# Two-request attention and gMLP encoder: rotary score passes over 128 rows, s tiles in natural order, weight sums spread differently

## The chip, the cores and the metric

The kernel runs on one core of one Trainium2 chip. The time is that of one execution on the device in microseconds (us); the median of several runs is given. The engines of the core work side by side: TensorE (PE in the profile), VectorE (DVE), ScalarE (ACT), GpSimd (POOL), and SyncE (SP), whose queue issues every DMA of this kernel. Each executes its own instructions strictly in the order in which they were written into its queue.

## The reference

Two batches, a sample of 1024 tokens and a prompt of 512 tokens (1024 features each), go through the same two layers. The first layer is multi-head latent attention, the second a gated MLP with a spatial product over chunks of 128 tokens. All is float32.

```python
def mla_layer(x, g, w_in, q_norm, kv_norm, w_q_up, w_kv_up, w_out):
    h = rmsnorm(x, g)
    q_lat, kv_lat, k_rope, gate = jnp.split(h @ w_in, [384, 640, 704], axis=-1)
    q = (rmsnorm(q_lat, q_norm) @ w_q_up).reshape(bsz, seq, 8, 128 + 64)
    kv = (rmsnorm(kv_lat, kv_norm) @ w_kv_up).reshape(bsz, seq, 8, 128 + 128)
    q_rope, k_rope = apply_rope(q[..., 128:], cos, sin), apply_rope(k_rope, cos, sin)
    s = einsum('bqhd,bkhd->bhqk', q_nope, k_nope) + einsum('bqhr,bkr->bhqk', q_rope, k_rope)
    o = einsum('bhqk,bkhd->bqhd', softmax(s * scale), v)
    return x + (o * silu(gate)) @ w_out

def gmlp_layer(x, g, w_in, ln_g, ln_b, w_s, b_s, w_out):
    u, v, gate = jnp.split(rmsnorm(x, g) @ w_in, 3, axis=-1)
    u, v = gelu(u), layernorm(gelu(v), ln_g, ln_b)
    s = u * (einsum('gpq,bnqgd->bnpgd', w_s, v_chunks) + b_s)
    return x + (s * silu(gate)) @ w_out
```

A final RMSNorm follows. The rotary part of a key has 64 features and is shared by the 8 heads.

## The kernel before

**Numbers and products.** Features lie on the partitions and tokens along the free axis. Every float32 operand x of a large product is split into a high part (`split`: a copy by ACT in the rounded type fp32r) and a low part (x minus the high part, by DVE), and a product is made as three matmuls, high*high, high*low and low*high, which add up in one PSUM bank (`mm3`). A matmul has 128 contracted rows and 512, 384 or 256 columns.

**Stages.** In the order of time: the sample's in-projection, the sample's attention (from about 180 us), the prompt's in-projection (about 575 to 660 us), the prompt's attention (to about 770 us), the two attention outputs, and then the gMLP twice, for two groups G=0 and G=1 of 768 tokens each. In a group the products with the weights follow a scheme in which operand blocks are added and subtracted first, and fewer block products are made. Its sums of the weight blocks `wv` are prepared by `w_sums`, eight units (two halves vu, four kt): a unit loads 1 MB into the tile `ws` (`load`, L847), makes four DVE subtractions or additions of 128x512 (`make`, L853) and stores 1 MB to DRAM (L234). Four units (vu=0) lie in the prompt's in-projection, one unit for each two steps of that stage; the other four lie in the attention output.

**Order.** There is no automatic scheduler in this program: each stage is a list of steps written by hand, and extra steps are woven in at positions by number. The order in which steps are called is the order on every engine. `Weights.reach` (L55, L63, L64) loads and splits weights a given number of steps ahead. The function `pin` returns its argument and does nothing else. Buffers are tiles of pools; a tile that lies where an earlier tile lay waits until the last use of the earlier tile is over.

**Scores** (`scores`, L618 to L625). For a block of 128 queries and each of two halves of 512 score columns four matmuls are made over 128 rows: three for the 128 ordinary features, and a fourth for the rotary features, with `qr` holding the high part of the 64 rotary rows in one half of the partitions and the low part in the other, against `krh`, which holds the high key part in both halves. What is then missing is high query times low key, 64 rows only. It is made for both halves together at the end: two matmuls of 64 rows, on rows 0 to 63 and on rows 64 to 127. Since an odd half needs the high part in the other partitions, `qrx` keeps a swapped copy (L582, ACT, 24 copies of 64 rows). The tables cos and sin are loaded by each rotary step (`p_qr`, L561).

**Rotary key of the prompt** (`evac`, f=5): kr from PSUM (L354), loads of cos and sin (L356, L357), four DMAs that shuffle kr into `rope` (L361), kr*cos (L362), rope*sin (L363), their sum (L364), then split into krh and krl.

**Norms in the prompt's in-projection.** Two sums of squares are turned into scales by matmuls on a tile of ones (`ones_mm`, L179 and L180: high part sh, low part sl). The scale is put on a diagonal (`norm_d`, L193, tile `dg`) and split in turn, so that PE waits for ACT's `sh<-dg` and DVE's `sl<-dg`.

**s tiles.** At the end of a group its 16 products s (one for each 128 features, d = 0 to 15) go to DRAM from the tiles `uo` (L234, `sd<-uo`), come back for 512 tokens at a time (L1182), and are split into sh and sl (L1191 by ACT, L1192 by DVE) for the output product (`out`, L1271 to L1273), which takes d in rising order. Tiles 0 to 2 have space of their own. For tiles 3 to 15 space is handed out by `open_out` in this order:

```python
        n = NPRE[G]
        for d in (*range(n + 3, n + 12), *range(n, n + 3), *range(n + 12, 16)):
            s_tiles(G, d)
```

With n = 3 that is 6 to 14, then 3, 4, 5, then 15. The first nine pairs lie where the pool `h2b` was (the split inputs gbh, gbl of the last weight products L1007 to L1009), the later ones where the pool `pu` was, that is the tiles `uo`.

Of the kernel before, what the change touches and what calls it, by code (L numbers as in the profile page):

```python
# [9 lines left out]
F32 = mybir.dt.float32  # L10
# [78 lines left out]
def trunk_kernel(tc, A):  # L89
# [146 lines left out]
    def pin(ins):  # L236

        return ins
# [13 lines left out]
    def setup():  # L252
# [8 lines left out]
        dve.memset(ones[:, :128], 1.0)  # L261
        st["onesr"] = const.tile([128, 128], F32R, name="onesr")
# [250 lines left out]
    def attention(b, n_ch):  # L513
# [5 lines left out]
        def begin():  # L519
            st["at", b] = open_pool("att" + b)  # L520
# [28 lines left out]
        def p_qr(p, c):  # L549
            cc = slice(c * C, (c + 1) * C)  # L550

            def f1():
# [5 lines left out]
                for nm in ("cos", "sin"):  # L558
                    st[nm] = tmp(nm) if n_ch == 1 else st["at", b].tile(
                        [128, C], F32, tag=nm, bufs=1, name=nm)  # L560
                    nc.sync.dma_start(out=st[nm], in_=A[nm][:, cc])  # L561
# [6 lines left out]
            def f2():  # L568
                qx, qs = st["qx"], st["qs"]
                dve.tensor_tensor(out=qx, in0=qx, in1=st["cos"], op=ALU.mult)  # L570
                dve.tensor_tensor(out=qs, in0=qs, in1=st["sin"], op=ALU.mult)

            def f3():
                qr = st["qx"]
                dve.tensor_tensor(out=qr, in0=qr, in1=st["qs"], op=ALU.add)

                x = st["qrx", p, c] = st["at", b].tile([128, C], F32R, tag="qrx", bufs=n_ch, name="qrx")
                for e in range(2):
# [3 lines left out]
                    act.copy(x[o:o + 64], qr[s:s + 64])  # L582
# [21 lines left out]
        def scores(i):  # L604
# [3 lines left out]
            last = []  # L608
            for j2 in range(2):
# [230 lines left out]
    def w_sums(u):  # L840


        vu, kt = divmod(u, 4)

        def load():
            t = st["wsum", u] = st["ws"].tile([128, 4, C], F32, tag="ws", bufs=2 - vu, name="ws")
            nc.sync.dma_start(out=t, in_=A["wv"][vu][:, :, kt, :])  # L847

        def make():
            t = st.pop(("wsum", u))  # L850
            for r, a, b, op in ((3, 2, 3, ALU.add), (2, 0, 2, ALU.subtract),
                                (0, 3, 0, ALU.subtract), (1, 1, 0, ALU.subtract)):
                pin(dve.tensor_tensor(out=t[:, r, :], in0=t[:, a, :], in1=t[:, b, :], op=op))  # L853
            store(st["Sv", vu][:, :, kt, :], t)
# [55 lines left out]
    def b_prep(G):  # L910
# [4 lines left out]
        def load(k):  # L915
            def fn():
                Q[k] = st["hq"].tile([128, 4, H], F32, name=f"hQ{k}")
                for j in range(2):
                    pin(nc.sync.dma_start(out=Q[k][:, j:j + 3:2, :], in_=st["x1d", G, k + 4 * j].rearrange(
                        "p (a b) -> p a b", a=2)))  # L920
# [30 lines left out]
        def first(k):  # L951
            def fn():
                q = Q[k]
                for j in range(2):
                    pin(dve.scalar_tensor_tensor(
                        out=q[:, j:j + 3:2, :], in0=q[:, j:j + 3:2, :],
                        scalar=vec(V_NG1 + k + 4 * j), in1=st["rbc1", G],
                        op0=ALU.mult, op1=ALU.mult))
# [5 lines left out]
        def second(k):  # L964
            def fn():
                q = Q[k]
                dve.tensor_tensor(out=q[:, 2, :], in0=q[:, 3, :], in1=q[:, 2, :], op=ALU.subtract)
# [4 lines left out]
        def third(k):  # L972
            def fn():
                q = Q[k]
                x = tmp("t1")[:, :H].unsqueeze(1)
                dve.tensor_tensor(out=x, in0=q[:, 3:4, :], in1=q[:, 0:1, :], op=ALU.subtract)
# [11 lines left out]
        def fifth(k):  # L988
            def fn():
                q = Q[k]  # L990
                dve.tensor_tensor(out=q[:, 1, :], in0=q[:, 1, :], in1=q[:, 0, :], op=ALU.subtract)
# [91 lines left out]
    def b_ug(G, early):  # L1083
# [4 lines left out]
        def norm_v(p):  # L1088
            def fn():
                v = st["vin", p]  # L1090
                for tt in range(6):
                    pin(dve.tensor_scalar(
                        out=v[:, tt, :], in0=v[:, tt, :], scalar1=st["mv"][:, tt, 0:1],
                        scalar2=st["mv"][:, tt, 3:4], op0=ALU.subtract, op1=ALU.mult))
# [90 lines left out]
    def s_split(g, d):  # L1185
        def fn():
# [4 lines left out]
            pin(act.copy(hi, x))  # L1191
            pin(dve.tensor_tensor(out=lo, in0=x, in1=hi.bitcast(F32), op=ALU.subtract))  # L1192
# [8 lines left out]
    def b_out(g, extra, last):  # L1201
# [24 lines left out]
        def fin4(f):  # L1226
            y = st["yl", f]
            pin(dve.scalar_tensor_tensor(out=y, in0=y, scalar=vec(V_FG + f), in1=st["bc0"],
# [372 lines left out]
```

## Time and profile before

| what | before |
|---|---|
| median of 3 runs | 1959.8 us (1959.45 to 1960.33) |
| the profiled execution | 1958.94 us |
| its span, first to last instruction | 1957.2 us |
| PE busy | 1922.0 us (98%) |
| DVE busy | 1290.7 us (66%) |
| ACT busy | 903.3 us (46%) |
| POOL busy | 147.8 us (8%) |
| moved by DMA | 274.13 MB, mean 140 GB/s |
| mean granted clock of PE | 0.996 |

Busy times are shares of the span, and engines overlap. Matmuls overlap each other too: a matmul of 512 columns is drawn as 0.39 us, and the next one starts 0.23 us after it. So the distance between the starts of two matmuls, not their durations, tells what one costs.

### The profile page before, as it was taken

What the parts mean: (1) busy time and instruction counts of PE and PEld (TensorE: products, weight loads), DVE (VectorE), ACT (ScalarE), POOL (GpSimd) and SP (SyncE); (2) the same over time, 40 slices, a digit from 0 to 9 for tenths busy, and PEclk for the clock granted to TensorE, in tenths of its full rate; (3) what the DMA queues carried; (4) which work ended last, traced back from release to release, by engine and by line L of the source; (5) the groups of instructions that cost most, each with busy time, mean ns of one, the idle gap of its engine ahead of it and who ended that gap; (6) DMA issues with size and microseconds to landing.
All of it is one profiled execution on the core that took longest, in us unless ns stands there. A gap on an engine that the chain in (4) does not pass through costs nothing.

```text
span 1957.2 us, 26572 instructions
## 1 busy us (share of the span) xinstructions
PE 1922.0 (98%) x10226; PEld 1672.0 (85%) x10226; DVE 1290.7 (66%) x1958; ACT 903.3 (46%) x1406; POOL 147.8 (8%) x99
## 2 busy tenths in 40 slices
PE   8999999999999999999999999999999999999998
PEld 6888788888887788888889999988878999997887
DVE  7443877777776788638757877766665666556443
ACT  5322545455562565424645445453544454544321
POOL 4200000000021000123000000002100000000111
PEclk9999999999999999999999999999999999999999
DMA  4211100010116312477556655456485555436443
GB/s 162 86 38 57 33 30 27 28 34 28 44 49 227 126 62 71 159 262 234 187 165 230 215 188 189 162 187 217 151 272 193 192 184 170 164 129 218 166 163 102
DMA packets 121518, 274.13 MB, mean 140 GB/s; under 512 B 12208, under 2 KB 40368, under 8 KB 121392
## 3 DMA queue, kind: packets, MB, share of 16 engines
q1 hardware_dynamic: 121392, 272.45, 42.2%
q8 instruction: 80, 1.31, 0.3%
q14 instruction: 46, 0.38, 0.1%
HBM read 203.45 MB, written 65.01 MB: 137 GB/s over the span
## 4 chain that ended last, share of the span: by engine, by line
PE 85%; DVE 8%; DMA 4%; issue 1%; ACT 1%; SPq 0%; POOL 0%; DVEq 0%; POOLq 0%; ACTq 0%
PE mm L145 7%; PE mm L147 7%; PE mm L146 7%; PE s L618 7%; PE X L1007 6%; PE X L1008 6%; PE X L1009 6%; PE mm L1272 4%; PE mm L1273 4%; PE mm L1271 4%; PE pst L656 3%; PE Z L1007 3%; PE Z L1008 3%; PE Z L1009 3%; PE o L145 2%; PE sv L1141 2%
## 5 line engine op out<-in xcount | busy, mean ns | idle before, releaser
L63 ACT CAST w_hi<-w_raw 128x1024 fp32r<-128x1024 f32 (+3 forms) x267 | 260.7, 977 | 390.8 <-PE mm L1272 102.4
L64 DVE TENSOR_TENSOR w_lo<-w_raw,w_hi 128x1024 fp32r<-128x1024 f32 (+3 forms) x267 | 304.1, 1140 | 190.1 <-ACT w_hi L63 185.9
L225 POOL TENSOR_TENSOR acc<-acc,sq 128x512 f32<-128x512 f32 x70 | 122.9, 1758 | 1444.9 <-ACT sq L223 556.3
L1272 PE MATMUL mm<-sl,w_hi 128*128 128x512 f32 (+1 forms) x416 | 156.1, 375 | 4.4 <-DVE sl L1192 4.4
L1273 PE MATMUL mm<-sh,w_lo 128*128 128x512 f32 (+1 forms) x416 | 155.8, 374 | 0.0
L1271 PE MATMUL mm<-sh,w_hi 128*128 128x512 f32 (+1 forms) x416 | 155.1, 374 | 0.0
L639 ACT ACTIVATE p<-s,sm 128x1024 f32<-128x1024 f32 (+1 forms) x96 | 93.2, 974 | 96.4 <-DVE sm L635 93.6
L150 ACT CAST pth<-pst 128x512 fp32r<-128x512 f32 x160 | 86.3, 590 | 66.6 <-PE pst L656 65.8
L145 PE MATMUL mm<-h_hi,w_hi 128*128 128x512 f32 x288 | 114.7, 398 | 1.0 <-ACT rbc L328 0.9
L146 PE MATMUL mm<-h_lo,w_hi 128*128 128x512 f32 x288 | 113.1, 393 | 0.0
L147 PE MATMUL mm<-h_hi,w_lo 128*128 128x512 f32 x288 | 113.1, 393 | 0.0
L151 DVE TENSOR_TENSOR ptl<-pst,pth 128x512 fp32r<-128x512 f32 x160 | 104.8, 683 | 9.7 <-ACT pth L150 9.1
L633 DVE TENSOR_REDUCE sm<-s 128x1 f32<-128x1024 f32 (+1 forms) x80 | 97.5, 1218 | 19.3 <-PE s L625 19.0
L1017 ACT COPY t<-X 128x384 f32<-128x384 f32 (+1 forms) x88 | 44.3, 509 | 125.1 <-PE X L1009 121.8
L145 PE MATMUL o<-pth,vh 128*128 128x256 f32 x320 | 95.0, 297 | 0.0
L1272 PEld LDWEIGHTS mm<-sl,w_hi 128*128 128x128 f32 x416 | 78.7, 189 | 18.9 <-DVE sl L1192 5.2
L1271 PEld LDWEIGHTS mm<-sh,w_hi 128*128 128x128 f32 x416 | 78.8, 189 | 13.9
L1273 PEld LDWEIGHTS mm<-sh,w_lo 128*128 128x128 f32 x416 | 78.8, 189 | 13.9
L146 PE MATMUL o<-ptl,vh 128*128 128x256 f32 x320 | 90.6, 283 | 0.0
L147 PE MATMUL o<-pth,vl 128*128 128x256 f32 x320 | 90.2, 282 | 0.0
L1007 PE MATMUL X<-gbh,w_hi 128*128 128x384 f32 x256 | 85.9, 335 | 2.1 <-DVE uo L1107 2.1
L1007 PE MATMUL X<-gah,w_hi 128*128 128x384 f32 x256 | 87.0, 340 | 0.0
(295 smaller groups left out, 5128.3 us busy)
## 6 DMA issues: line engine op xcount, KB each, us to landing
w_raw<-wbo SPq DMA_DIRECT2D x50, 512.0 KB, 3.4
w_raw<-wug SPq DMA_DIRECT2D x48, 512.0 KB, 4.3
w_raw<-sv SPq DMA_DIRECT2D x32, 512.0 KB, 3.5
su<-su SPq DMA_DIRECT2D x32, 512.0 KB, 4.6
w_raw<-su SPq DMA_DIRECT2D x32, 512.0 KB, 4.5
w_raw<-wa SPq DMA_DIRECT2D x25, 512.0 KB, 3.6
w_raw<-wv SPq DMA_DIRECT2D x24, 512.0 KB, 3.5
v2d<-c SPq DMA_DIRECT2D x48, 256.0 KB, 2.6
```

The source lines that it names most:

```text
L63: self.nc.scalar.copy(hi[:, :n], raw[:, :n])
L64: self.nc.vector.tensor_tensor(out=lo[:, :n], in0=raw[:, :n], in1=hi[:, :n].bitcast(F32), op=ALU.subtract)
L145: pe.matmul(out, lh, rh, start=(i == 0), stop=False)
L146: pe.matmul(out, lh, rl, start=False, stop=False)
L147: pe.matmul(out, ll, rh, start=False, stop=(i == n - 1))
L618: pe.matmul(s[:, j2 * C:(j2 + 1) * C], l[:, o], r[:, cc], start=(j == 0), stop=False)
L1007: pe.matmul(ps, lh, rh, start=first, stop=False, skip_group_check=True)
L1008: pe.matmul(ps, lh, rl, start=False, stop=False, skip_group_check=True)
L1009: pe.matmul(ps, ll, rh, start=False, stop=last, skip_group_check=True)
L1271: pe.matmul(ps, wh[:, ksl(kk)], sh, start=(k == 0), stop=False)
L1272: pe.matmul(ps, wh[:, ksl(kk)], sl, start=False, stop=False)
L1273: pe.matmul(ps, wl[:, ksl(kk)], sh, start=False, stop=(k == 15))
```

## The change

Five edits are made.

1. `scores`: the missing rotary product is made with 128 rows like the others, `(qr, krl)`, for each half in its turn. The pair of 64-row matmuls, the tile `qrx` and its 24 copies go. The low rows of `qr` times `krl` are added to the result, which the form before left out.
2. cos and sin are loaded once for each request when its attention begins (128x1024 and 128x512), instead of in each of the 12 rotary steps.
3. `open_out` hands out the s tiles in the order 3 to 15.
4. `w_sums` takes a unit's place and width as arguments. Three of the four vu=0 units stay in the prompt's in-projection, one for each three steps with the sums three steps after the load; the fourth is cut into four quarters of 128 columns, woven into the prompt's attention at steps 1+3i (load) and 3+3i (sums and store), each with a single buffer. The vu=1 units keep their order.
5. `setup` starts with 16 matmuls of 128 columns on a tile of ones, into a PSUM tile that nobody reads.

The diff also takes `pin` away in some places and puts it in others, and s_split calls `split` instead of the same two instructions; neither changes an instruction. Its core:

```diff
+        idle = mm_tile("idle")
+        for _ in range(16):
+            pe.matmul(idle[:, :128], ones[:, :128], ones[:, :128], start=True, stop=True)
...
-            st["at", b] = open_pool("att" + b)
+            ap = st["at", b] = open_pool("att" + b)
+            for nm in ("cos", "sin"):
+                st[nm] = ap.tile([128, T], F32, name=nm)
+                nc.sync.dma_start(out=st[nm], in_=A[nm][:, :T])
...
-                x = st["qrx", p, c] = st["at", b].tile([128, C], F32R, tag="qrx", bufs=n_ch, name="qrx")
...
-                    act.copy(x[o:o + 64], qr[s:s + 64])
...
-                terms = [(qh, kh), (qh, kl), (ql, kh), (qr, st["krh", b])]
+                terms = [(qh, kh), (qh, kl), (ql, kh), (qr, st["krh", b]), (qr, st["krl", b])]
                 for j, (l, r) in enumerate(terms):
                     pe.matmul(s[:, j2 * C:(j2 + 1) * C], l[:, o], r[:, cc],
-                              start=(j == 0), stop=False)
-
-                rows = slice(64 * j2, 64 * j2 + 64)
-                hi = qr if j2 == h % 2 else st["qrx", h // 2, c]
-                last.append((s[:, j2 * C:(j2 + 1) * C], hi[rows, o], st["krl", b][rows, cc]))
-            for out, l, r in last:
-                pe.matmul(out, l, r, start=False, stop=True)
+                              start=(j == 0), stop=(j == 4))
...
-            sums_at(n, 0, 2)
+                sums_at = sums_steps([(0, 0), (0, 1), (0, 2)], 0, 3, 3)
+            for f in sums_at.get(n, ()):
+                step(f)
...
+    quarters = [w_sums(0, 3, 1, ksl(i)) for i in range(4)]
+    weave.append((0, lambda: st.update(ws=open_pool("ws", side="right"))))
+    for i, (load, make) in enumerate(quarters):
+        weave += [(1 + 3 * i, load), (3 + 3 * i, make)]
+    weave.append((13, lambda: close_pool("ws")))
...
-        n = NPRE[G]
-        for d in (*range(n + 3, n + 12), *range(n, n + 3), *range(n + 12, 16)):
+        for d in range(NPRE[G], 16):
             s_tiles(G, d)
```

What stands in the queues at three places follows. Line numbers of the changed kernel differ by a few: L846 there is L853 before, L840 is L847, L351 is L347, L360, L361 and L365 are L356, L357 and L361, L366 to L368 are L362 to L364, L378 is L374.

DVE in the prompt's in-projection, behind the third unit's sums and as far as the split of the first scale (`sl<-dg`), before:

```order
L64 TENSOR_TENSOR w_lo<-w_raw,w_hi 128x1024
L186 TENSOR_TENSOR dg<-ps_n,ident 128x512
L188 TENSOR_REDUCE ms<-dg 128x4
L163 TENSOR_SCALAR ms<-ms 128x4
L853 TENSOR_TENSOR ws<-ws 128x512
L193 TENSOR_TENSOR dg<-ident,rstd 128x512
L853 TENSOR_TENSOR ws<-ws 128x512 x3
L362 TENSOR_TENSOR kr<-kr,cos 128x512
L363 TENSOR_TENSOR rope<-rope,sin 128x512
L64 TENSOR_TENSOR w_lo<-w_raw,w_hi 128x1024
L364 TENSOR_TENSOR kr<-kr,rope 128x512
L151 TENSOR_TENSOR sl<-dg,sh 128x512
```

And in the changed kernel, over the same stretch:

```order
L64 TENSOR_TENSOR w_lo<-w_raw,w_hi 128x1024
L186 TENSOR_TENSOR dg<-ps_n,ident 128x512
L188 TENSOR_REDUCE ms<-dg 128x4
L163 TENSOR_SCALAR ms<-ms 128x4
L193 TENSOR_TENSOR dg<-ident,rstd 128x512
L64 TENSOR_TENSOR w_lo<-w_raw,w_hi 128x1024
L366 TENSOR_TENSOR kr<-kr,cos 128x512
L367 TENSOR_TENSOR rope<-rope,sin 128x512
L368 TENSOR_TENSOR kr<-kr,rope 128x512
L151 TENSOR_TENSOR sl<-dg,sh 128x512
```

The fourth unit's four sums are gone from between the scale's steps; a weight split has moved ahead of the rotary steps.

SP's queue in the same stage (`wa`, `wh`, `wp` are weights, `sv` the store of a unit), before:

```order
L847 DMA ws<-wv 128x4x512
L55 DMA w_raw<-wa 128x1024
L356 DMA cos<-cos 128x512
L357 DMA sin<-sin 128x512
L55 DMA w_raw<-wa 128x1024
L847 DMA ws<-wv 128x4x512
L361 DMA rope<-kr 32x512 x4
L55 DMA w_raw<-wh 128x640
L234 DMA sv_5565<-ws 512x1x512
```

And in the changed kernel:

```order
L840 DMA ws<-wv 128x4x512
L55 DMA w_raw<-wa 128x1024
L360 DMA cos<-cos 128x512
L361 DMA sin<-sin 128x512
L55 DMA w_raw<-wa 128x1024
L234 DMA sv_5530<-ws 512x1x512
L365 DMA rope<-kr 32x512 x4
L55 DMA w_raw<-wh 128x640
L527 DMA cos<-cos 128x512
L527 DMA sin<-sin 128x512
```

The fourth load is gone, and the third unit's store now stands ahead of the four shuffles into `rope` instead of behind them.

DVE at the end of the group G=0: the splits of s tiles 3 to 7, with the tiles' numbers, which rise in the order in which space is handed out. Before:

```order
L1155 TENSOR_TENSOR uo_11761<-uo_11761,uo_11930 128x768
L1192 TENSOR_TENSOR sl_12018<-s_11922,sh_12017 128x512
L1192 TENSOR_TENSOR sl_12020<-s_11945,sh_12019 128x512
L1192 TENSOR_TENSOR sl_12022<-s_11961,sh_12021 128x512
L1192 TENSOR_TENSOR sl_12000<-s_11982,sh_11999 128x512
L1192 TENSOR_TENSOR sl_12002<-s_11984,sh_12001 128x512
```

And in the changed kernel:

```order
L1148 TENSOR_TENSOR uo_11727<-uo_11727,uo_11896 128x768
L151 TENSOR_TENSOR sl_11966<-s_11888,sh_11965 128x512
L151 TENSOR_TENSOR sl_11968<-s_11911,sh_11967 128x512
L151 TENSOR_TENSOR sl_11970<-s_11927,sh_11969 128x512
L151 TENSOR_TENSOR sl_11972<-s_11948,sh_11971 128x512
L151 TENSOR_TENSOR sl_11974<-s_11950,sh_11973 128x512
```

The instructions stand in the same order; what changed is that the first three write to places that were handed out first (in the former h2b) instead of tenth to twelfth (in the former uo tiles).

## Rows read from the trace of the kernel before

**Rows 1.** The page, engines' busy time and the chain of waits.

```profile
PE 1922.0 (98%) x10226; PEld 1672.0 (85%) x10226; DVE 1290.7 (66%) x1958; ACT 903.3 (46%) x1406; POOL 147.8 (8%) x99
...
PE 85%; DVE 8%; DMA 4%; issue 1%; ACT 1%; SPq 0%; POOL 0%; DVEq 0%; POOLq 0%; ACTq 0%
```

**Rows 2.** Timeline of PE at 561 us: start, duration, line, operation.

```profile
561.80 0.39 PE L618 MATMUL s<-krh,qr 128*128 128x512 f32 x1
...
562.12 0.50 PE L625 MATMUL s<-krl,qr 64*128 64x512 f32 x1
562.55 0.39 PE L145 MATMUL o<-pth,vh 128*128 128x256 f32 x1
```

**Rows 3.** Line L625: PE's idle time before it, by what ended it (us, times).

```profile
  issue: 28.5, 80
```

**Rows 4.** Timeline of PE at the end of G=0; brackets: idle before, releaser.

```profile
1303.27 0.40 PE L1272 MATMUL mm<-sl,w_hi 128*128 128x512 f32 x1
...
1308.94 0.39 PE L1271 MATMUL mm<-sh,w_hi 128*128 128x512 f32 x1
1311.31 0.50 PE L1272 MATMUL mm<-sl,w_hi 128*128 128x512 f32 x1 [1.98 <-DVE sl L1192]
```

**Rows 5.** Timeline of DVE at the end of G=0.

```profile
1305.00 0.69 DVE L1192 TENSOR_TENSOR sl<-s,sh 128x512 fp32r<-128x512 f32 x1
1310.57 2.50 DVE L1192 TENSOR_TENSOR sl<-s,sh 128x512 fp32r<-128x512 f32 x4 [4.87 <-DMA sd<-uo]
```

**Rows 6.** Timeline of PE at the end of G=1.

```profile
1771.10 0.39 PE L1271 MATMUL mm<-sh,w_hi 128*128 128x512 f32 x1
1773.87 0.80 PE L1272 MATMUL mm<-sl,w_hi 128*128 128x512 f32 x1 [2.38 <-DVE sl L1192]
...
1777.39 0.40 PE L1271 MATMUL mm<-sh,w_hi 128*128 128x512 f32 x1
```

**Rows 7.** Timeline of PE in the prompt's in-projection.

```profile
631.77 0.39 PE L147 MATMUL mm<-h_hi,w_lo 128*128 128x512 f32 x1
634.23 0.49 PE L179 MATMUL ps_n<-sh,onesr 128*128 128x512 f32 x1 [2.08 <-ACT sh L150]
...
644.16 0.39 PE L145 MATMUL mm<-h_hi,w_hi 128*128 128x512 f32 x1
```

**Rows 8.** Timeline of DVE in the prompt's in-projection.

```profile
629.58 0.69 DVE L853 TENSOR_TENSOR ws<-ws 128x512 f32<-128x512 f32 x1 [3.00 <-DMA ws<-wv]
...
630.79 2.13 DVE L853 TENSOR_TENSOR ws<-ws 128x512 f32<-128x512 f32 x3
...
635.79 0.68 DVE L151 TENSOR_TENSOR sl<-dg,sh 128x512 fp32r<-128x512 f32 x1
```

**Rows 9.** Timeline of POOL in the same stage.

```profile
626.65 1.02 POOL L166 TENSOR_TENSOR rstd<-ms,mhalf 128x4 f32<-128x4 f32 x1 [12.58 <-DVE ms L163]
```

**Rows 10.** Timeline of SP's queue in the same stage.

```profile
621.07 3.21 SPq L361 DMA_DIRECT2D rope<-kr  x4
...
625.45 0.60 SPq L234 DMA_DIRECT2D sv<-ws  x1
```

**Rows 11.** Tile rope: time of its DMAs from issue to landing.

```profile
DMA to landing us min/median/max: 2.0/3.3/8.7
```

**Rows 12.** Page, DMA issues: count, KB each, median us to landing.

```profile
sv<-ws SPq DMA_DIRECT2D x8, 1024.0 KB, 5.5
```

**Rows 13.** Windows: length, busy of PE, PEld, DVE, ACT, POOL (instructions), clock, DMA, GB/s.

```profile
631.00:646.00 15.00, 10.62 (x31) 7.21 (x29) 13.99 (x22) 6.78 (x10) 0.86 (x1) 0.77 0.35 122
680.00:708.00 28.00, 28.00 (x149) 22.39 (x150) 26.88 (x51) 20.32 (x43) 0.00 (x0) 1.00 0.23 72
1770.00:1779.00 9.00, 6.62 (x22) 5.03 (x21) 3.13 (x5) 3.12 (x5) 0.00 (x0) 0.81 0.57 191
```

**Rows 14.** Line L151, 128x128: DVE durations in ns (min, median, max).

```profile
L151 DVE TENSOR_TENSOR w0lo<-w0raw,w0hi x24: 275/279/1384, 3.9 to 25.9; 128x128 fp32r<-128x128 f32 x24
```

**Rows 15.** Timeline of PE at the program's start.

```profile
5.79 0.79 PE L422 MATMUL mm<-h_hi,w0hi 128*128 128x512 f32 x1 [5.79 <-ACT h_hi L305]
```

More of the change, by code (lines that the diff above doesn't have):

```diff
@@ L557, in f1 @@
                          for k in range(3)])
[L558 to L561, printed above, removed]
                 qx, qs = st["qx"], st["qs"] = tmp("qx"), tmp("qs")
@@ L569, in f2 @@
                 qx, qs = st["qx"], st["qs"]
-                dve.tensor_tensor(out=qx, in0=qx, in1=st["cos"], op=ALU.mult)
-                dve.tensor_tensor(out=qs, in0=qs, in1=st["sin"], op=ALU.mult)
+                dve.tensor_tensor(out=qx, in0=qx, in1=st["cos"][:, cc], op=ALU.mult)
+                dve.tensor_tensor(out=qs, in0=qs, in1=st["sin"][:, cc], op=ALU.mult)
             def f3():
@@ L838, in sums, with w_sums @@
             dve.tensor_tensor(out=o[r], in0=a, in1=b, op=op)
[L840 to L843 removed]
+    def w_sums(vu, kt, bufs=2, o=slice(0, C)):
+        q = []
         def load():
[L846 to L847 removed]
+            q.append(st["ws"].tile([128, 4, o.stop - o.start], F32, tag="ws", bufs=bufs, name="ws"))
+            nc.sync.dma_start(out=q[0], in_=A["wv"][vu][:, :, kt, o])
         def make():
[L850 removed]
+            t = q.pop()
             for r, a, b, op in ((3, 2, 3, ALU.add), (2, 0, 2, ALU.subtract),
                                 (0, 3, 0, ALU.subtract), (1, 1, 0, ALU.subtract)):
[L853 to L854 removed]
+                dve.tensor_tensor(out=t[:, r, :], in0=t[:, a, :], in1=t[:, b, :], op=op)
+            store(st["Sv", vu][:, :, kt, o], t)
         return load, make
@@ L966, in fn @@
                 q = Q[k]
[L967 removed]
+                pin(dve.tensor_tensor(out=q[:, 2, :], in0=q[:, 3, :], in1=q[:, 2, :], op=ALU.subtract))
                 dve.tensor_tensor(out=q[:, 0, :], in0=q[:, 2, :], in1=q[:, 0, :], op=ALU.add)
@@ L975, in fn @@
                 x = tmp("t1")[:, :H].unsqueeze(1)
-                dve.tensor_tensor(out=x, in0=q[:, 3:4, :], in1=q[:, 0:1, :], op=ALU.subtract)
+                pin(dve.tensor_tensor(out=x, in0=q[:, 3:4, :], in1=q[:, 0:1, :], op=ALU.subtract))
                 split_to(k, "ga", 3, x)
@@ L990, in fn @@
                 q = Q[k]
-                dve.tensor_tensor(out=q[:, 1, :], in0=q[:, 1, :], in1=q[:, 0, :], op=ALU.subtract)
+                pin(dve.tensor_tensor(out=q[:, 1, :], in0=q[:, 1, :], in1=q[:, 0, :], op=ALU.subtract))
                 split_to(k, "gb", 2, q[:, 1:2, :])
@@ L1190, in fn @@
             x = st.pop(("sraw", g, d))
-            pin(act.copy(hi, x))
-            pin(dve.tensor_tensor(out=lo, in0=x, in1=hi.bitcast(F32), op=ALU.subtract))
+            split(hi, lo, x)
         return fn
@@ L1315, in b_out, with sums_steps @@
         return [fin0, fin1, fin2], [[lambda f=f, fn=fn: fn(f) for f in range(KD)] for fn in (fin3, fin4)]
-    w_sums_of = [w_sums(u) for u in range(8)]
-    def sums_at(n, u0, every):
-        u, i = divmod(n, every)
-        if i == 0 and 0 <= u < 4:
-            step(w_sums_of[u0 + u][0])
-        u, i = divmod(n - 2, every)
-        if i == 0 and 0 <= u < 4:
-            step(w_sums_of[u0 + u][1])
+    def sums_steps(units, first, every, lag):
+        at = {}
+        for i, u in enumerate(units):
+            load, make = w_sums(*u)
+            at.setdefault(first + int(i * every) + lag, []).append(make)
+            at.setdefault(first + int(i * every), []).append(load)
+        return at
     def steps(lst):
@@ L1375, in trunk_kernel @@
     step(open_out1)
+    sums_at = sums_steps([(1, kt, 1) for kt in range(4)], 3, 3, 2)
     for h in range(KD):
@@ L1381, in trunk_kernel @@
                 step(lambda f=f, c=c: out_s.out(f, c), ("wao", f))
-                sums_at(2 * f + c - 3, 4, 3)
+                for e in sums_at.get(2 * f + c, ()):
+                    step(e)
                 if 2 * f + c == 14:
```

17 lines of the change are left out of this document (8 added, 9 removed).

## The prediction

> **What bounds the kernel now.** I began with the page: PE is busy 98% of the span and makes 85% of the chain that ended last [rows 1]. So only what takes time out of PE's stream, or a hole in it, counts; DVE and ACT count where PE waits for them. Since matmuls overlap, I then measured PE by the distances between starts. At full rate the output product goes from 1303.27 to 1308.94 in 25 steps, 5.67 us, or 0.227 us a matmul of 512 columns [rows 4]. Everything longer than that is excess, and the timelines show three kinds that this change touches: a short gap at each of the 80 score pairs [rows 2, 3], a hole at the end of each gMLP group [rows 4, 6], and a hole in the prompt's in-projection [rows 7]. After two of the holes the granted clock is below full (mean 0.86 and 0.81 in those windows [rows 13]), so that the hole costs more than its own length.
>
> **Part 1, scores.** Removed are 80 pairs of 64-row matmuls, added are 160 matmuls of 128 rows. Now the last full matmul before a pair starts at 561.80, the pair at 562.12, the next full matmul at 562.55 [rows 2]: 0.75 us for the full one and the pair. PE sat idle before each pair for a reason that is only called issue, 28.5 us over 80 pairs, 0.36 each [rows 3]. In the changed kernel the same work is three full matmuls, 3 x 0.227 = 0.68. Saved: 0.07 us x 80 = 5.6 us. With 0.23 a matmul it is 4.8; I keep 4 to 6 as the bounds. The 24 copies for qrx and the repeated loads of cos and sin go too, but ACT and DMA are not on the chain (1% and 4% [rows 1]), so that is worth nothing.
>
> The Trainium skill (TensorEngine Tiling (Array Packing), Theoretical Speedup) says that two tiles of 64 rows give up to twice the rate; by that the pair costs one slot, and its removal would cost, not save. The same page (Key Properties) says that a change of the tiling mode drains the engine; the gap of 0.36 us before every pair agrees with that.
>
> **Part 2, s tiles.** In G=0 PE starts a high product at 1308.94 and the next one, with sl, at 1311.31: 2.37 us instead of 0.23, waiting for DVE's split [rows 4]. DVE had split tile 3 at 1305.00 and then waited 4.87 us, until 1310.57, for the DMA that stores uo [rows 5]: the tile's place is a former uo tile. In G=1 the wait is 1771.10 to 1773.87, 2.77 us, and then eight steps to 1777.39 take 3.52 us instead of 1.81, at half clock [rows 6]. Excess: 2.14 + 2.54 + 1.71 = 6.4 us. In natural order tiles 3 to 11 lie where h2b was, whose last readers are the weight products that end before the output product begins; the tiles that must wait for uo are 12 to 15, which PE wants some 10 us later. DVE then runs tiles 3 to 7 one after the other from 1305.0 at about 0.6 us each (four in 2.50 [rows 5]): tile 4 is there at 1306.3, where PE wants it at 1309.2, and what comes next, hQ and a weight split, has over 2 us to spare. So all of it goes: 6.4 us, bounds 4 and 6.8.
>
> **Part 3, the prompt's in-projection.** From 631.77 to 644.16 PE makes 17 steps of 512 columns [rows 7]: 12.39 us, where 17 x 0.227 = 3.86. The excess is 8.5 us. It begins with PE waiting for ACT's sh(dg) and DVE's sl(dg), the split of the scale. The scale itself is known at 627.7 (POOL, 626.65 + 1.02 [rows 9]). But DVE's next instruction is the fourth unit's first sum, which waits 3.00 us for its load; it and the three behind it take 0.69 and 2.13 us, and sl(dg) comes at 635.79 only [rows 8]. In the changed kernel these sums and their load are elsewhere. DVE makes dg at 627.7 to 628.4, a weight split to 629.6, kr*cos to 630.2; that frees the slot for which sh(dg) waited, and ACT has sh(dg) at about 630.9, before PE is at 632.0. Then rope*sin, the sum and sl(dg), 0.6 each: about 632.2 if rope has landed by 630.2. The second scale's sl(acc) follows three instructions later, at 634.0. PE then has four norm products made at about 634.2 instead of 632.9: a rest of 1.3 us, and I put 1.8 for it, since the rope's DMAs move behind the third unit's 1 MB store. Those were issued from 621.07 and now follow a store that waits for the third unit's sums, so from about 624.6; they landed in 3.3 us in the median and 8.7 at most [rows 10, 11]. I expect them near 630, not at once, because the store before them takes 5.5 us [rows 12]. A hole of 1 to 2 us in two pieces should not bring the half clock: the 2.14 us in G=0 did not [rows 4]. Gain 8.5 - 1.8 = 6.7 us, bounds 3 and 7.5.
>
> **Part 4, the quarters.** The fourth unit's 16 sums of 128x128 now run in the prompt's attention. A DVE operation of this shape takes 0.28 us [rows 14]: 4.5 us of DVE. PE is fully busy there and DVE is busy 26.88 of 28.00 us [rows 13]. In such a window about two quarters fall, 2.2 us, which is 1.1 us over what is free. Softmax runs a block ahead of PE, which takes up most of it; a single buffer adds waits of the next load for the last store on SP, with weight loads behind it, and DVE waits in its order if a load is late, with the softmax of the next block behind it. Between 0 and 4.5 us I take 0.7, nearer to 0, because DVE has free time in the rest of the attention.
>
> **Part 5, the start and the rest.** The products on ones run before PE's first matmul at 5.79, which waits for ACT [rows 15]. They can raise the clock of the first matmuls, or reach a little past 5.79. The next waits of PE there are again for data, so either effect is mostly taken back: 0, bounds -0.5 and +1. Small moves of score blocks against transposes and projections: 0, +-1.5.
>
> **Sum.** -5.6 - 6.4 - 6.7 + 0.7 = -18.0 us. Against the profiled execution's 1958.94 that is 1940.9. The median of the runs is 1959.8, 0.9 above the profiled one, so I predict 1941.8.
>
> **Rivals.**
>
> *The rope is late.* The store ahead of the four shuffles makes them land at the far end of what was seen, 8.7 us [rows 11] after some 627, thus 635 to 636, and rope*sin holds DVE, with sl(dg) behind it. PE then waits about as long as now, and the clock falls again. For it: the 1 MB before them in the same queue. Against it: the stage moves 1 MB of loads and one store less. Then part 3 gains 1 us instead of 6.7: 1947.5. Chance 0.13.
>
> *The uo store still ends last.* If the tiles that DVE wants next wait for something else that ends as late (the raw s, or the last readers of h2b), part 2 gains nothing: 1948.2. Against it: in both groups the wait is put down to the store, and the split of tile 3 ran at 1305.00 without one. Chance 0.06.
>
> *The quarters hold DVE.* If each quarter's sums wait 3.0 us for their load, as the fourth unit's did [rows 8], and PE pays for all of it, that is 12 us: 1958.9 - 18.7 + 12 = 1952.2, with 0.9 for the median 1953.1. Against it: the loads are 256 KB instead of 1 MB, issued two steps ahead, in a window in which DMA is busy 0.23 [rows 13]. Chance 0.05.
>
> *Slower: the gap is not the pair's.* The two 64-row matmuls do start together [rows 2]. If the 0.32 us ahead of them belonged to something that stays (the first use of krl, say), the change would put two full matmuls where one slot is: at most +0.227 x 80 = +18.1 us instead of -5.6, so 1958.9 + 18.1 - 12.4 = 1964.6, with 0.9 for the median 1965.5. It decides the sign from 0.2 us for each pair, since the other parts give 12.4 and 0.2% (3.9 us, about what can be told from no change here) come on top. Against it: the wait is there 80 times, before the pairs only, and the pair itself holds PE 0.43 us, nearly two slots. Chance 0.03. The packing rule of the Trainium skill cited above would give this time.
>
> *It does not do what it says.* The edits to pin change no instruction and are worth 0 in any case; this is in the forecast.
>
> **How the numbers follow.** The forecast, all parts about as worked out, has 0.70. Its own ends are 1958.94 - 20.3 + 0.9 = 1939.5 with all the upper bounds (6, 6.8, 7.5, nothing for the quarters), about 1.5 less with the small moves, and some 1946 with a part near its lower bound. The first two rivals end at 1947.5 and 1948.2, or 2 us higher with part 1 at its lower bound. The range 1938 to 1951 takes these in and leaves out the quarters, the slower case, and any two failures together. Within 0.2% means 1955.9 to 1963.7: it takes two rivals at once, or quarters worse than their row. Faster 0.93, same 0.04, slower 0.03.
>
> **What would show it.** Part 1: no gap called issue in the scores, steps of 0.23 throughout. Part 2: no wait of DVE for the uo store between 1305 and 1310 (some 12 us earlier in the new trace), and no drop of the clock in G=1. Part 3: DVE's dg right behind the scale, the first norm product without a long wait, full clock to the end of the stage; wrong if rope*sin waits for DMA or the half clock is there again. Part 4: PE without holes in the prompt's attention. The prediction is wrong if one of the last two shows a new wait of more than 5 us, or if the score blocks do not get shorter.

## The result and the profile after

The changed kernel takes 1947.1 us (median of 4 runs, 1945.2 to 1948.8) against 1959.6 (1957.9 to 1960.3) before, a ratio of 0.9933 with a 95% interval of 0.9918 to 0.9949. In a second comparison (`e9_changed_again` below) it was 1947.5 against 1961.4, a ratio of 0.9926 (0.9914 to 0.9938). The forecast was 1941.8, in a range of 1938 to 1951. So the sign and the range hold, and some 5 us of the forecast gain are missing. The profiled execution took 1948.76 us.

The page of the changed kernel, engines' busy time and chain of waits, answers to [rows 1]:

```profile
PE 1917.7 (98%) x10258; PEld 1698.2 (87%) x10258; DVE 1287.1 (66%) x1970; ACT 889.7 (46%) x1382; POOL 148.1 (8%) x99
...
PE 84%; DVE 8%; DMA 5%; issue 1%; ACT 1%; SPq 0%; POOL 0%; DVEq 0%; POOLq 0%; ACTq 0%
```

It looks as before. What helps is to cut the timeline of PE at the first and last product of each stage and to compare the lengths (us, worked out from those starts; the last column is the changed kernel without the products on ones, `e1_no_idle` below):

| stretch of PE | before | changed | without products on ones |
|---|---|---|---|
| span's start to the first score | 189.9 | 189.6 | 189.9 |
| sample's attention, to the prompt's first in-projection product | 386.2 | 378.9 | 378.7 |
| prompt's in-projection, to its last product | 100.7 | 96.9 | 93.9 |
| prompt's attention, to the first output product | 112.2 | 110.9 | 111.0 |
| attention outputs | 137.3 | 138.7 | 137.3 |
| last output product to the first X | 0.2 | 4.9 | 0.2 |
| G=0 to its first output product | 375.1 | 376.6 | 375.6 |
| output product of G=0 | 89.2 | 87.3 | 88.1 |
| G=1 to its first output product | 373.0 | 373.8 | 375.6 |
| to the last product | 186.2 | 182.3 | 182.3 |

The three stages that the prediction named got shorter. One place nobody had named got longer: between the last attention output product and the first product X of the gMLP. PE's waits in the changed kernel, by what they waited for (us in total, times, longest), begin with it:

```profile
PE X L1000 <- DVE x L772: 4.5, 1, 4.5
PE X L1000 <- DVE uo L1100: 2.5, 3, 1.3
PE ps_n L180 <- DVE sl L151: 1.8, 4, 0.8
```

The timeline of PE in the changed kernel shows the place, and the half clock behind it (0.43 us a step until 925.07):

```profile
915.01 0.39 PE L147 MATMUL mm<-goh,w_lo 128*128 128x512 f32 x1
919.88 0.77 PE L1000 MATMUL X<-w_hi,gah 128*128 128x512 f32 x1 [4.48 <-DVE x L772]
920.44 0.63 PE L1001 MATMUL X<-w_lo,gah 128*128 128x512 f32 x1
...
924.71 0.52 PE L1002 MATMUL X<-w_hi,gal 128*128 128x512 f32 x1
925.07 0.39 PE L1000 MATMUL X<-w_hi,gah 128*128 128x512 f32 x1
```

In the kernel before, PE went over from one to the other without a pause:

```profile
926.30 0.39 PE L147 MATMUL mm<-goh,w_lo 128*128 128x512 f32 x1
926.53 0.39 PE L1007 MATMUL X<-w_hi,gah 128*128 128x512 f32 x1
```

DVE's instruction that the first X waits for (L772, before L779) adds the last output product to x. It stands as late in both, 4.05 us behind the start of PE's last output product:

```profile
919.06 0.67 DVE L772 TENSOR_TENSOR x<-mm,x 128x512 f32<-128x512 f32 x1
```

```profile
930.35 0.67 DVE L779 TENSOR_TENSOR x<-mm,x 128x512 f32<-128x512 f32 x1
```

So nothing is slower; PE has begun to wait for it. The first X has no use for x. What it needs is room in PSUM. The output products and the X, Y, Z products use pools of four buffers each, and the pools lie on the same banks. In the built programs the last output product has bank 1 before and bank 0 in the changed kernel, and the first X has bank 0 in both. (It is no plain rotation: the last four output products have banks 2, 3, 0, 1 before and 1, 3, 2, 0 in the changed kernel.) The difference is the tile `idle` for the products on ones: it takes one buffer at the very start, and all later tiles of that pool come to lie otherwise. By these rows the hole costs 4.87 - 0.23 = 4.6 us and the half clock 5.19 - 12 x 0.227 = 2.5 (12 steps from 919.88 to 925.07). In the table the two stretches behind the last output product are 6.1 us longer together, since other small waits in the stretch of G=0 differ from kernel to kernel (against e1 and e2 below the two stretches are 5.6 and 6.4 us longer).

A correction belongs here. The part ahead of the prediction says that there is no scheduler and that the order of calls is the order on every engine. The rows of the order that stand there say otherwise: the third unit's sums, called with the tenth step of the stage, are queued ahead of kr*cos, which is called six steps sooner. The framework that builds the program puts an instruction into its queue where it reckons it to be ready, and hands out the buffers that are free at that point. So one more tile at the start changes buffers 900 us later.

The prompt's in-projection in the changed kernel, DVE (answers to [rows 8]):

```profile
614.61 2.87 DVE L846 TENSOR_TENSOR ws<-ws 128x512 f32<-128x512 f32 x4 [4.73 <-DMA ws<-wv]
...
621.28 0.69 DVE L193 TENSOR_TENSOR dg<-ident,rstd 128x512 f32<-128x512 f32 x1 [1.13 <-POOL rstd L166]
...
623.46 0.69 DVE L366 TENSOR_TENSOR kr<-kr,cos 128x512 f32<-128x512 f32 x1 [0.36 <-DMA rope<-kr]
...
625.40 0.69 DVE L151 TENSOR_TENSOR sl<-dg,sh 128x512 fp32r<-128x512 f32 x1
```

and PE (answers to [rows 7]):

```profile
624.12 0.39 PE L147 MATMUL mm<-h_hi,w_lo 128*128 128x512 f32 x1
624.86 0.50 PE L179 MATMUL ps_n<-sh,onesr 128*128 128x512 f32 x1 [0.35 <-ACT sh L150]
626.14 0.50 PE L180 MATMUL ps_n<-sl,onesr 128*128 128x512 f32 x1 [0.78 <-DVE sl L151]
626.84 0.51 PE L179 MATMUL ps_n<-sh,onesr 128*128 128x512 f32 x1 [0.21 <-ACT sh L150]
627.94 0.76 PE L180 MATMUL ps_n<-sl,onesr 128*128 128x512 f32 x1 [0.59 <-DVE sl L151]
```

The hole of 4.5 us (at 634.23 and 636.52 in the kernel before) has become four holes from 624.12 to 627.94, 2.9 us over what these four steps need, and the clock falls again, 0.83 and 0.88 in the two windows (columns as in [rows 13]):

```profile
624.00:630.00 6.00, 4.07 (x11) 2.08 (x10) 5.97 (x11) 5.04 (x7) 0.00 (x0) 0.83 0.53 181
630.00:636.00 6.00, 6.00 (x25) 4.89 (x24) 4.67 (x8) 2.31 (x5) 1.01 (x1) 0.88 0.08 5
```

At the ends of G=0 and G=1 both waits for the uo store are gone, and PE is busy at full clock throughout (windows that reach from the uo sums to past the old waits):

```profile
1296.00:1306.00 10.00, 10.00 (x47) 8.32 (x45) 6.69 (x9) 4.25 (x8) 0.00 (x0) 1.00 0.81 261
1757.50:1772.00 14.50, 14.50 (x66) 12.00 (x65) 9.54 (x14) 8.21 (x14) 0.00 (x0) 1.00 0.78 241
```

DVE splits s tiles 3 to 7 in one go, right behind uo, as against [rows 5]:

```profile
1299.60 3.09 DVE L151 TENSOR_TENSOR sl<-s,sh 128x512 fp32r<-128x512 f32 x5
```

### The profile page after: what moved, and what is told of

The parts are those of the page before. It is cut to its first block, busy times and chain, and to the rows that moved or that the text cites. A ratio compares the mean times of both kernels' runs of the same rounds, so it can differ in the third digit from the quotient of the medians.

```text
span 1947.0 us, 26592 instructions
## 1 busy us (share of the span) xinstructions
PE 1917.7 (98%) x10258; PEld 1698.2 (87%) x10258; DVE 1287.1 (66%) x1970; ACT 889.7 (46%) x1382; POOL 148.1 (8%) x99
## 4 chain that ended last, share of the span: by engine, by line
PE 84%; DVE 8%; DMA 5%; issue 1%; ACT 1%; SPq 0%; POOL 0%; DVEq 0%; POOLq 0%; ACTq 0%
PE s L617 9%; PE mm L145 6%; PE mm L146 6%; PE mm L147 6%; PE X L1000 6%; PE X L1001 6%; PE X L1002 6%; PE mm L1264 4%; PE mm L1263 4%; PE mm L1265 4%; PE pst L649 3%; PE Z L1000 3%; PE Z L1001 3%; PE Z L1002 3%; PE sv L1134 2%; PE o L146 2%
## 5 line engine op out<-in xcount | busy, mean ns | idle before, releaser
L145 PE MATMUL mm<-h_hi,w_hi 128*128 128x512 f32 x288 | 114.3, 397 | 1.0 <-ACT rbc L332 0.9
L151 DVE TENSOR_TENSOR ptl<-pst,pth 128x512 fp32r<-128x512 f32 x160 | 104.6, 681 | 8.2 <-ACT pth L150 8.1
L145 PE MATMUL o<-pth,vh 128*128 128x256 f32 x320 | 90.6, 283 | 0.0
```

The lines of the kernel that those rows point to most:

```text
L145: pe.matmul(out, lh, rh, start=(i == 0), stop=False)
```

## The experiments

The experiments were timed in three groups, each with the kernel before beside it: e1 to e4 (before: 1961.0 us), e5 to e7 (1961.1) and e8 and e9 (1961.4). Single runs of one kernel spread over several us (1958.4 to 1965.0 for the kernel before in the first group), and the intervals of the ratios are 2 to 3 us to either side. The kernel without products on ones (e1, 1940.5 us) is the base for e2 and e4 to e7; e5 to e7 are compared with it across groups. A difference of a few us between two medians is therefore rough, and where the stretches of the traces say more, they are given too.

**e1, the products on ones taken out of the changed kernel.**

```diff
-        idle = mm_tile("idle")
-        for _ in range(16):
-            pe.matmul(idle[:, :128], ones[:, :128], ones[:, :128], start=True, stop=True)
```

> The changed kernel without the 16 products on ones and their PSUM tile. In the changed kernel the first X product waits 4.5 us for DVE's sum out of the last output product (x L772), at half clock for the next 5 us. Theory (bank): the tile `idle` takes one turn of the four PSUM buffers, so that the rotation ends one place further, and the first X gets the very bank of the last output product, where before it got the one before. Without the tile the wait is gone: 6 us less than the changed kernel, about 1941 us. Rival (pace): PE has become some 11 us earlier and runs into DVE there whatever the bank; then nothing changes, about 1947. A third part: the products themselves (warm-up); if they help, the start gets up to 1 us longer, and the first product comes at 5.8 again instead of 7.4.

Measured: 1940.45 us, ratio 0.9895 (0.9882 to 0.9908), 6.6 less than the changed kernel's 1947.1. In the built program the last output product is on bank 1 again, and the first X follows it at once:

```profile
910.69 0.39 PE L147 MATMUL mm<-goh,w_lo 128*128 128x512 f32 x1
910.92 0.39 PE L997 MATMUL X<-w_hi,gah 128*128 128x512 f32 x1
```

PE is even earlier here than in the changed kernel (910.7 against 915.0), and does not wait. The pace is not the cause.

**e2, the same 16 products in four tiles.**

```diff
-        idle = mm_tile("idle")
-        for _ in range(16):
-            pe.matmul(idle[:, :128], ones[:, :128], ones[:, :128], start=True, stop=True)
+        for r in range(4):
+            idle = mm_tile("idle")
+            for _ in range(4):
+                pe.matmul(idle[:, :128], ones[:, :128], ones[:, :128], start=True, stop=True)
```

> The changed kernel with the same 16 products on ones, four each into four PSUM tiles, so that the rotation makes a whole turn. Bank theory: the first X does not wait, the time is that of the kernel without products within 0.5 us, about 1941. Pace theory, or the products themselves as the cause: the wait of 4.5 us stays, about 1947.

Measured: 1939.44 us, ratio 0.9890 (0.9876 to 0.9904). The products stay, the wait is gone, the last output product is on bank 1. So it is where the tiles lie, not the products. What the products themselves are worth cannot be told: the first score starts at 189.1 to 189.7 in the five traces with them and at 189.5 to 189.9 in the six without, and the medians of e1 and e2 differ by less than their scatter.

**e3, the products on ones (one tile) added to the kernel before.**

```diff
+        idle = mm_tile("idle")
+        for _ in range(16):
+            pe.matmul(idle[:, :128], ones[:, :128], ones[:, :128], start=True, stop=True)
```

> The kernel before with nothing but the 16 products on ones added (one PSUM tile). Bank theory: the first X, which starts at 926.5 right behind the last output product in the kernel before, now waits for DVE's last sum (930.35 + 0.67), 4.6 us, and falls to half clock: about 6 us slower than before, 1965.7. Pace theory: before, PE is not early, nothing changes: 1959.6, give or take 1 us for the start.

Measured: 1965.79 us against 1961.02, ratio 1.0025 (1.0016 to 1.0035): 4.8 slower. The last output product is on bank 0, and the wait appears in a kernel that had none:

```profile
924.59 0.39 PE L147 MATMUL mm<-goh,w_lo 128*128 128x512 f32 x1
929.48 0.76 PE L1011 MATMUL X<-w_hi,gah 128*128 128x512 f32 x1 [4.50 <-DVE x L783]
```

**e4, the old order of s tiles in e1.**

```diff
-        for d in range(NPRE[G], 16):
+        n = NPRE[G]
+        for d in (*range(n + 3, n + 12), *range(n, n + 3), *range(n + 12, 16)):
             s_tiles(G, d)
```

> The kernel without products on ones, with the s tiles handed out in the old order (6 to 14, 3 to 5, 15). If the order is what removed the waits for the uo store, both waits come back (2.1 us in G=0, 2.5 and 1.7 us of half clock in G=1): 5.8 to 6.4 us above the kernel without products, about 1947. If the waits went for another reason (PE and DVE having moved against each other): no difference.

Measured: 1946.75 us, 6.3 above e1 (by the two output stretches of the traces 1.4 and 4.1, together 5.5). Both waits are back, here in PE and in DVE at the end of G=0:

```profile
1295.00 0.50 PE L1261 MATMUL mm<-sl,w_hi 128*128 128x512 f32 x1 [2.32 <-DVE sl L151]
```

```profile
1294.25 1.93 DVE L151 TENSOR_TENSOR sl<-s,sh 128x512 fp32r<-128x512 f32 x3 [5.21 <-DMA sd<-uo]
```

**e5, the 64-row pairs back in e1**, with qrx, its copies, and cos and sin loaded by each rotary step:

```diff
-                terms = [(qh, kh), (qh, kl), (ql, kh), (qr, st["krh", b]), (qr, st["krl", b])]
+                terms = [(qh, kh), (qh, kl), (ql, kh), (qr, st["krh", b])]
...
+            for out, l, r in last:
+                pe.matmul(out, l, r, start=False, stop=True)
```

> The kernel without products on ones (1940.5 us), with the 64-row pairs, qrx and its copies, and the loads of cos and sin by each rotary step put back. Theory of the prediction: the pair costs 0.07 us more than two full matmuls, 80 times: +5.6 us, 1946. Theory from the trace of the changed kernel: the full matmul behind the pair pays too (the o products in the sample's attention took 91.9 us before and 89.1 now, the s products 156.0 and 153.4, the transposes 52.2 and 51.0): 7.3 us for 64 pairs, 1.3 for 16, together +8.5, 1949. By the packing rule the pair costs half of two full ones: -18 us, 1922.

Measured: 1949.67 us, 9.2 above e1: near the second theory, above the first, and against the packing rule. In its trace the idle time ahead of the pairs is what it was in [rows 3]:

```profile
  issue: 28.5, 80
```

**e6, all four units of sums back in the prompt's in-projection of e1, no quarters.**

```diff
-                sums_at = sums_steps([(0, 0), (0, 1), (0, 2)], 0, 3, 3)
+                sums_at = sums_steps([(0, 0), (0, 1), (0, 2), (0, 3)], 0, 2, 2)
...
-    quarters = [w_sums(0, 3, 1, ksl(i)) for i in range(4)]
```

> The kernel without products on ones, with all four vu=0 units back in the prompt's in-projection, one for each two steps, and no quarters. DVE's order there is again that of the kernel before. Theory: the hole there returns whole (8.5 us of excess instead of about 1.5), and the quarters in the prompt's attention cost next to nothing (the attention's PE stretch is not longer with them): +6 to +7 us, 1946.5 to 1947.5. Rival: the quarters do cost (0.7 or more) and part of the gain in the stage is paid back: +3 to +5.

Measured: 1946.24 us, 5.8 above e1, between the two expectations. DVE's queue is the old one, and so is the hole:

```profile
625.62 0.51 PE L179 MATMUL ps_n<-sh,onesr 128*128 128x512 f32 x1 [1.26 <-ACT sh L150]
627.90 0.62 PE L180 MATMUL ps_n<-sl,onesr 128*128 128x512 f32 x1 [1.78 <-DVE sl L151]
```

The in-projection takes 99.6 us here and 93.9 in e1, 5.7 more; the prompt's attention 110.2 without quarters and 111.0 with them. The four quarters cost 0.8 us. The attention outputs are 1.5 us longer in this trace than in e1's, so that the 5.8 is not the stage alone.

**e7, eight quarters in the prompt's attention** (three tiles for the products on ones, so that the banks of the last output product and the first X differ):

```diff
-                sums_at = sums_steps([(0, 0), (0, 1), (0, 2)], 0, 3, 3)
+                sums_at = sums_steps([(0, 0), (0, 1)], 0, 3, 3)
...
-    quarters = [w_sums(0, 3, 1, ksl(i)) for i in range(4)]
+    quarters = [w_sums(0, 2 + i // 4, 1, ksl(i % 4)) for i in range(8)]
...
-        weave += [(1 + 3 * i, load), (3 + 3 * i, make)]
+        weave += [(i * 3 // 2, load), (i * 3 // 2 + 2, make)]
```

> Spread thinner still: only two vu=0 units in the prompt's in-projection, the third and the fourth as eight quarters of 128 columns in the prompt's attention (two for each three steps, one buffer). The 16 products on ones go into three PSUM tiles, so that the last output product and the first X have different banks, as in the kernel with four tiles (1939.4 us). It doubles the DVE work and the DMAs that the change added to the attention. Theory: what is left of the hole in the in-projection (1.2 to 1.8 us, 4.9 in the profile of the changed kernel) comes from the third unit's sums waiting for their load, and goes; the attention hides eight quarters as it hid four: 1938. Rival: quarters cost PE time, so that eight cost what four do once more (0.7 or more) and weight loads come late behind stores on SP's queue: 1940 to 1943.

Measured: 1940.56 us, ratio 0.9886 (0.9869 to 0.9902), no better than e2. One half of each theory holds: the in-projection is 1.6 us shorter than in e2 (92.5 against 94.1, its hole is gone), and the attention 3.4 us longer (114.3 against 110.9). There PE now waits for DVE, as at this place:

```profile
747.15 0.66 PE L650 MATMUL pst<-ident,p 128*128 128x128 f32 x4 [0.54 <-DVE ql L151]
748.34 0.39 PE L146 MATMUL o<-ptl,vh 128*128 128x256 f32 x1 [0.54 <-DVE ptl L151]
```

The cost of sums in the attention is not in proportion: 0.8 us for the first four quarters, 3.4 for the next four. DVE's time is not used up: it is busy 101.2 of 114.2 us, against 97.2 of 110.9 in e2. What is new is that DVE waits for the quarters' loads, 4.6 us in five waits (0.2 in one wait in e2), with the work that PE needs queued behind them:

```profile
DVE ws L847 <- DMA ws<-wv: 4.6, 5, 1.3
739.08 0.94 DVE L847 TENSOR_TENSOR ws<-ws 128x128 f32<-128x128 f32 x3 [1.32 <-DMA ws<-wv]
```

PE's waits for DVE in the attention come to 2.7 us here and 0.2 in e2. That the late loads are the whole of the 3.4 us is not shown; no run gave the eight quarters a second buffer or an earlier load.

**e8, the kernel before with only the score pairs replaced.**

```diff
-                terms = [(qh, kh), (qh, kl), (ql, kh), (qr, st["krh", b])]
+                terms = [(qh, kh), (qh, kl), (ql, kh), (qr, st["krh", b]), (qr, st["krl", b])]
...
-            for out, l, r in last:
-                pe.matmul(out, l, r, start=False, stop=True)
```

> The kernel before with one edit: the 64-row pairs replaced by matmuls of 128 rows (qrx and its copies go; cos and sin are still loaded by each rotary step). The prediction's price (0.07 us for each of 80 pairs) gives -5.6; the price that the removal showed in the changed kernel (9.2) gives -8.5 to -9, some of which can be lost behind it, where PE waits for the same loads and stores as before (the two uo waits and the hole in the in-projection stay): -8.

Measured: 1953.14 us against 1961.43, ratio 0.9950 (0.9936 to 0.9964): -8.3. In its trace the sample's attention is 7.5 us shorter than in the kernel before and the prompt's, which has no quarters here, 2.0; the attention outputs are 1.6 longer. The copies for qrx come and go with the pairs in both runs; that the time is lost at the pairs is read from the starts (below).

**e9, the changed kernel once more.**

> The changed kernel once more, for a second trace. In its first one the third unit's load landed at 614.6 us, its sums held DVE until 617.4, and PE lost 4.9 us in the prompt's in-projection, half clock among them; in the four kernels with the same schedule of sums the landing was 611.2 to 613.1 and the loss 1.2 to 2.1. If that is this execution's DMA alone, the loss is now 1 to 3 us, while the wait of 4.5 us at the first X and the half clock behind it are there unchanged. If it belongs to the changed kernel (the other PSUM buffers of its norm products), it is again 4 to 5 us.

Measured: 1947.51 us. The wait at the first X is there unchanged (914.30 to 919.18). In the prompt's in-projection the third unit's load landed at 613.8, the holes came to 2.3 us and the half clock came again; the stretch took 96.5 us. That is nearer to the second expectation than to the first. Counted from the start of the stage the sums could begin at 46.1 and 45.5 us in the two traces of the changed kernel, and at 43.0 to 44.8 in the four kernels with the same sums and other banks (e1, e2, e4, e5), whose stretch took 93.3 to 94.1 us. Two traces against four: whether the other banks have a part in it, or it is chance in that DMA's time, stays open.

## Why the prediction was right, and where it was off

The forecast against the stretches of the two profiles (us; before to changed):

| part | forecast | measured |
|---|---|---|
| both attentions: scores and quarters | -5.6 + 0.7 = -4.9 | -7.3 - 1.3 = -8.6 |
| prompt's in-projection | -6.7 | -3.8 |
| s tiles: the two output products of the gMLP | -6.4 | -1.9 - 3.9 = -5.8 |
| first X, and G=0 behind it | 0 | +6.1 |
| attention outputs | 0 | +1.4 |
| start, G=1 | 0 | -0.3 + 0.8 = +0.5 |
| sum | -18.0 | -10.2 |

**Scores.** Right in place and sign, too small: 5.6 us forecast, 8.3 (e8) and 9.2 (e5) measured, 7.3 + 1.3 in the two stretches of the table (the second with the quarters in it). The step that was off is the price of a pair, taken up to the start of the next full matmul. That matmul pays too. The rows of the kernel before behind [rows 2] show it:

```profile
562.55 0.39 PE L145 MATMUL o<-pth,vh 128*128 128x256 f32 x1
562.77 0.28 PE L146 MATMUL o<-ptl,vh 128*128 128x256 f32 x1
562.89 0.27 PE L147 MATMUL o<-pth,vl 128*128 128x256 f32 x1
```

The first o product holds PE 0.22 us, the next one 0.12 (where a transpose follows the pair, it is 0.16 against 0.11). Now the same kind of place in the changed kernel, where 0.23 a score product goes over into 0.11 or 0.12 an o product without a gap:

```profile
554.63 0.39 PE L617 MATMUL s<-krh,qr 128*128 128x512 f32 x1
554.86 0.39 PE L617 MATMUL s<-krl,qr 128*128 128x512 f32 x1
555.09 0.28 PE L145 MATMUL o<-pth,vh 128*128 128x256 f32 x1
555.20 0.28 PE L146 MATMUL o<-ptl,vh 128*128 128x256 f32 x1
```

Summed by kind over the sample's attention the starts give 2.6 us less for the score products, 2.8 for the o products, 1.2 for the transposes and 0.7 for the rest. The change into 64 rows and the change back both cost. At this place a pair costs 0.09 us ahead of it (0.32 from the full matmul to the pair, instead of 0.23) and 0.10 behind it, and gains 0.02 itself (0.43 against 2 x 0.227). The prediction said that PE sat idle 0.36 us before each pair. That is a misreading of [rows 3], which changed nothing in the sum: the 28.5 us are idle time of PEld, PE's weight loads. Between two full matmuls of these rows a weight load runs during the matmul ahead of its own; at a pair, and at the full matmul behind it, it starts only together with its own matmul. The kernel before at the place shown above, and below it the first o product of the changed kernel, whose matmul starts at 555.09:

```profile
562.11 0.18 PEld L625 LDWEIGHTS s<-krl,qrx 64*128 64x128 f32 x1 [0.35 <-issue]
562.55 0.19 PEld L145 LDWEIGHTS o<-pth,vh 128*128 128x128 f32 x1 [0.25 <-issue]
```

```profile
554.86 0.19 PEld L145 LDWEIGHTS o<-pth,vh 128*128 128x128 f32 x1
```

The slower rival (the cost ahead of the pair stays) is refuted. The packing rule of the Trainium skill (TensorEngine Tiling (Array Packing), Theoretical Speedup), up to twice the rate for 64 rows, gave the wrong sign here: with one pair at a time the change into 64 rows and back costs more than the packing saves.

**s tiles.** 6.4 forecast; 6.3 by the medians of e4 and e1, 5.8 and 5.5 by the stretches; the mechanism is as told.

**In-projection.** 6.7 forecast for the stage, 5.7 measured by e6 and 6.8 by the stretch of e1, but 3.8 in the profile of the changed kernel and 4.1 in e9. The step that failed is the rest of 1.8 us in two pieces. In the changed kernel the holes came to 2.9 us (e9: 2.3), and with them the half clock, which the sum had taken to stay away. Where the holes came to 1.3 and 1.5 us (e1, e2), it did stay away. Two things made the holes longer than worked out. The sums of the third unit wait for their load (4.73 us) and everything on DVE stands behind them; in the sum the scale had its old time. And kr*cos overwrites kr, which the rope shuffles still read, so it waits for those DMAs (0.36 us at 623.46); the sum had only rope*sin wait. The rival of the late rope did not happen: that wait is 0.3 to 1.1 us in the changed kernel, e1, e2, e4, e5 and e9. (The prediction's mean clock of 0.86 in the old hole is a misreading too: [rows 13] has 0.77. Nothing was worked out from it.)

**Quarters.** 0.7 forecast, 0.8 measured by the stretches of e6 and e1. Beside the pairs the four quarters cost nothing: the prompt's attention takes 112.2 us in the kernel before without them and 112.2 in e5 with them. **Start.** 0 forecast; what was gained before the first score is within the scatter of the traces.

**What the sum lacked** is the first X: 5.6 to 6.4 us by the two stretches of the changed kernel against those of the kernel before, e1 and e2. The medians (6.6 by e1, 4.8 by e3) hold more than that. The changed kernel's trace is also 3.0 us longer than e1's in the in-projection and 1.4 in the attention outputs, and 1.8 shorter in G=1; in e3 the half clock in G=1 stayed away (see the last section). The prediction costed the products on ones by their time and called them nothing, and never asked which buffer their tile takes. The row to ask for was there: the first X followed PE's last output product at once, while DVE read that product out 4 us later, so that it rested on the banks being different. The two misses, 3 us too little for the scores and 6 too much here, offset in part. With the scores as forecast the changed kernel would have taken some 1950 us, just inside the range, whose cases did not include this one: that it held is in part luck.

Some of the gain was given back: the attention outputs took 138.7 us instead of 137.3, since PE waits for the statistics behind the loads of x (L179, 869.40). The stretch is longer in e6, e8 and e9 too (138.5 to 138.9), but not in e1 to e5 and e7 (137.3 to 137.7), in most of which PE comes to this place earlier than in the changed kernel. So it is not PE's pace; why the wait comes in some kernels only is open.

**A faster version.** e1 (1940.5), e2 (1939.4) and e7 (1940.6) beat both kernels; e2 is the changed kernel with nothing but its 16 products spread over four tiles. The three cannot be told apart.

## What to carry to other kernels

A new tile in a rotating pool is an edit to every later tile of it: where one stage hands over to another on the same PSUM banks, look up which bank the last tile of the one and the first of the other have, before and after. Price a change of matmul form up to the second instruction behind it, by the distances between starts. When sums are moved under another stage, see whether each load will have landed by the time its engine comes to it in the queue: four quarters cost 0.8 us here, and four more cost 3.4, with DVE waiting for their loads.

## What was not expected of the hardware

The half clock does not follow from the length of a hole alone. In the wait for the uo store in G=1, 2.5 us over a step's time in the kernel before [rows 6] and 2.6 in e4 brought it (clock 0.81 in [rows 13] and in e4), while 2.8 us at the same place in e3 did not:

```profile
1775.95 0.39 PE L1275 MATMUL mm<-sh,w_hi 128*128 128x512 f32 x1
1778.94 0.50 PE L1276 MATMUL mm<-sl,w_hi 128*128 128x512 f32 x1 [2.60 <-DVE sl L1196]
1779.27 0.39 PE L1277 MATMUL mm<-sh,w_lo 128*128 128x512 f32 x1
1779.51 0.40 PE L1275 MATMUL mm<-sh,w_hi 128*128 128x512 f32 x1
```

At the end of G=0 the same wait brought it in e8 (2.6 us) but not in e4 (2.5) or in the kernel before (2.1 [rows 4]). In the in-projection holes of 2.3 and 2.9 us in three and four pieces brought it (e9 and the changed kernel), and 1.3 and 1.5 us did not (e1, e2). So a gain that is counted with the clock it gives back is uncertain by that much, here 1.7 us for each place. And a pair of 64-row matmuls that runs side by side is dearer than two full ones, by 0.10 to 0.12 us (8.3 to 9.2 us for 80), counted with what follows it.
